# A decoder layer's first norm: x loaded first, its squares summed on PE, c spread by PE, zeros run through PE

## The chip, the core and the metric

The kernel runs on one core of one Trainium2 chip. The metric is the device time of one execution in microseconds. The engines are named as in the profile: PE (matrix products) with PEld (its weight loads), DVE (vector), ACT (activations), POOL (general), SP (which issues the DMAs).

## What is computed

One layer of a hybrid decoder, on 256 rows of width 2048 in float32, conditioned by a vector c:

```python
cond = silu(c)
mod = cond @ ada_w + ada_b                   # nine vectors of 2048: shift, scale, gate for three blocks
h = rmsnorm(x, g1) * (1 + sc1) + sh1
x = x + 0.5 * gt1 * (silu(h @ wg1) * (h @ wu1)) @ wd1          # FFN 1, inner width 5632
h = rmsnorm(x, g2) * (1 + sc2) + sh2
x = x + gt2 * mixer(h)                       # 8 attention heads beside 8 gated-delta heads
h = rmsnorm(x, g3) * (1 + sc3) + sh3
x = x + 0.5 * gt3 * (silu(h @ wg2) * (h @ wu2)) @ wd2          # FFN 2
out = rmsnorm(x, final_norm)
```

rmsnorm divides each row by the root of the mean of its squares plus 1e-6. The change touches only what comes ahead of FFN 1's first matmul: silu(c), the first columns of mod, and the first rmsnorm.

## The kernel before

x is held transposed: 128 partitions, 16 slices (KD) of 128 channels, 256 rows T in the free dimension.

**Weights.** All weight matrices are packed in the order of their use, in blocks of 8 tiles of 128x128 (`Stream.next`, line 84). A block is loaded by SP (`wraw`, line 91), rounded by ACT to float32r (`whi`, line 94), and DVE takes the remainder (`wlo`, line 97). Three buffers of each hold blocks, and a fourth one takes every fourth block of an FFN. The activations are split likewise into a high and a low part (`hs`), so that each product is made of three matmuls: high by high, high by low, low by high.

**Modulation columns.** `mod` is made column by column on DVE (`ada_col`, line 186): SP loads 128x2048 weights, 1 MB (`adaf` for the first four, which have buffers of their own, then `adat`), and one multiply-and-sum against `cs` (silu(c), spread over all partitions) gives one column of 128 values (line 204). The first 32 columns are the scale and the shift of norm 1 in turn, slice by slice. After the first ones they go between the blocks of weights, at a rate per block that the table `RATE` gives.

**The start.** SP issues c, `colt` (small constants, the identity and the ones among them), the first column, x in five parts, three more columns (lines 152 to 162), then the stream. POOL spreads c over the partitions in four pieces (line 175), and ACT takes the silu (line 176). Then come two columns (line 505 on), a load of the Sqrt table (line 240), the squares of x on ACT part by part (line 507), their sum over the slices on DVE down to two slices (lines 506 and 509), and `norm_rstd` (line 255): four fp32 matmuls against two columns of ones (`nsum`, line 261), the root on ACT, reciprocal and one correction on DVE, the result laid out as `rb` (line 275), and two matmuls with the identity which make of it a row on all partitions (`nrow`, line 276), copied by DVE (line 281). `modulate_one` (line 286) makes a slice of h: `ht` on DVE (line 289), shift and rounding on ACT (lines 291, 292, 295), the low part on DVE (lines 293, 296). It needs a scale column (`gains`, line 298) and a shift column.

**FFN 1's first half.** `gate_up_first` (line 400) makes products in chunks of slices k (0 to 1, 2 to 5, 6 to 15) for 28 pairs of gate and up tiles. In the first chunk, eight pairs do k = 0 (two blocks of weights), then k = 1 (two blocks), then the others pair by pair; ACT evacuates each pair's PSUM bank (line 436). The matmuls are those of lines 423 to 425 (`pgu`).

**Order.** A scheduler places the instructions of each engine into one fixed order, by readiness; each engine then works strictly through its list. `tc.issue_after(i)` keeps an instruction behind i in that order. `W.hold` and `W.held` are such marks for the first `wlo`.

## Time and profile before

| | |
|---|---|
| median of 3 runs | 2117.76 us (2116.71 to 2119.72) |
| the profiled execution's own time | 2118.8 us |
| its span in the trace | 2117.0 us |
| mean granted clock of PE | 0.989 |
| first matmul of FFN 1 (`pgu`) | at 27.03 us |
| first matmul with a `wlo` | at 32.36 us |

A row of the trace in order of time reads: start in us, duration in us, engine, line, operation, output<-inputs, shapes, count, and in brackets how long the engine had been idle before and what released it. A row of a stretch reads: from:to and its length, then the busy us and the instructions of PE, PEld, DVE, ACT and POOL, the granted clock of PE, the share of time in which the DMA engines were busy, and GB/s. A row of a group ends with its count, busy us, mean ns of one, and idle us before.

### The profile page before, as it was taken

The numbers are of one execution on the slowest core, as the hardware profiler recorded it, in microseconds if no ns is written. First come the engines' busy times: TensorE is split into PE (matmuls) and PEld (weight loads), VectorE is DVE, ScalarE is ACT, GpSimd is POOL, SyncE is SP. The second block draws the span as 40 slices with busy tenths as digits, with TensorE's granted clock in tenths as the row PEclk, the third lists the DMA queues.
The fourth block names the chain that finished last, engine by engine and source line by source line (L and its number), as shares of the span: only waits on it lengthen the run. The fifth ranks groups of instructions, "written<-read, shape, count | busy, mean of one in ns | idle before, by whom it ended". The sixth has DMA issues, their size and how long they took to land.

```text
span 2117.0 us, 32815 instructions
## 1 busy us (share of the span) xinstructions
PE 2042.3 (96%) x12530; PEld 1808.7 (85%) x12530; DVE 1604.4 (76%) x2580; ACT 1021.3 (48%) x1622; POOL 99.7 (5%) x113
## 2 busy tenths in 40 slices
PE   5999999999999998999999999999999999999997
PEld 4998999888888887788888888788888888888886
DVE  6899877888888878789888888776665555555554
ACT  5544444433444446565556654554444334444442
POOL 0000000000000020110101002100000000000011
PEclk9999999999999999999999999999999999999998
DMA  8989776999999884655555557576666556555553
GB/s 313 331 341 348 265 253 254 334 349 333 331 334 328 339 290 154 202 209 200 196 203 212 197 219 282 192 262 230 234 234 197 188 187 191 191 190 189 189 189 110
DMA packets 123582, 518.16 MB, mean 245 GB/s; under 512 B 13721, under 2 KB 15769, under 8 KB 104993
## 3 DMA queue, kind: packets, MB, share of 16 engines
q1 hardware_dynamic: 123426, 516.07, 69.3%
q8 instruction: 98, 1.61, 0.3%
q14 instruction: 58, 0.48, 0.1%
HBM read 511.81 MB, written 4.21 MB: 244 GB/s over the span
## 4 chain that ended last, share of the span: by engine, by line
PE 82%; DVE 9%; DMA 4%; issue 2%; ACT 2%; POOL 0%; DVEq 0%; SPq 0%; ACTq 0%
PE pd L353 15%; PE pg L353 10%; PE pu L353 10%; PE pd L354 8%; PE pp L353 6%; PE pu L354 5%; PE pg L354 5%; PE pgu L425 4%; PE pgu L423 3%; PE pgu L424 3%; PE pp L354 3%; DVE wlo L97 3%; PE po L353 2%; DVE adat L204 2%; DMA adat<-in_ada_dram 2%
## 5 line engine op out<-in xcount | busy, mean ns | idle before, releaser
L94 ACT CAST whi<-wraw 128x1024 fp32r<-128x1024 f32 x674 | 705.9, 1049 | 802.6 <-PE pd L353 220.7
L97 DVE TENSOR_TENSOR wlo<-wraw,whi 128x1024 fp32r<-128x1024 f32 x674 | 823.3, 1225 | 349.2 <-ACT whi L94 348.0
L353 PE MATMUL pd<-hid,whi 128*128 128x512 f32 x1408 | 492.2, 393 | 0.0
L354 PE MATMUL pd<-hid,wlo 128*128 128x256 f32 x1408 | 393.2, 279 | 0.3 <-DVE wlo L97 0.3
L204 DVE CUSTOM_DVE_ANT_0 adat<-adat,cs,colt 128x2048 f32<-128x2048 f32 x140 | 334.6, 2390 | 42.1 <-DMA adat<-in_ada_dram 41.5
L353 PE MATMUL pg<-hs,whi 128*128 128x512 f32 x960 | 339.9, 394 | 2.6 <-DVE hs L296 1.8
L353 PE MATMUL pu<-hs,whi 128*128 128x512 f32 x960 | 340.3, 395 | 0.0
L353 PEld LDWEIGHTS pd<-hid,whi 128*128 128x128 f32 x1408 | 263.7, 187 | 61.9 <-DVE hid L368 0.3
L353 PE MATMUL pp<-hs,whi 128*128 128x512 f32 x784 | 292.9, 407 | 1.8 <-DVE hs L296 1.8
L354 PE MATMUL pu<-hs,wlo 128*128 128x256 f32 x960 | 269.5, 281 | 0.0
L354 PE MATMUL pg<-hs,wlo 128*128 128x256 f32 x960 | 269.4, 281 | 0.0
L354 PEld LDWEIGHTS pd<-hid,wlo 128*128 128x128 f32 x1408 | 264.4, 188 | 0.7 <-DVE wlo L97 0.6
L423 PE MATMUL pgu<-hs,whi 128*128 128x256 f32 x896 | 255.9, 287 | 8.0 <-ACT whi L94 6.9
L425 PE MATMUL pgu<-hs,wlo 128*128 128x256 f32 x896 | 252.1, 287 | 7.3 <-DVE wlo L97 7.1
L424 PE MATMUL pgu<-hs,whi 128*128 128x256 f32 x896 | 255.1, 286 | 0.0
L354 PE MATMUL pp<-hs,wlo 128*128 128x256 f32 x784 | 230.1, 294 | 0.2 <-DVE wlo L97 0.2
L353 PEld LDWEIGHTS pg<-hs,whi 128*128 128x128 f32 x960 | 180.6, 188 | 44.1 <-issue 2.1
L353 PEld LDWEIGHTS pu<-hs,whi 128*128 128x128 f32 x960 | 180.6, 188 | 41.4
L354 PEld LDWEIGHTS pg<-hs,wlo 128*128 128x128 f32 x960 | 181.9, 189 | 0.5 <-DVE wlo L97 0.4
L423 PEld LDWEIGHTS pgu<-hs,whi 128*128 128x128 f32 x896 | 174.2, 195 | 9.4 <-ACT whi L94 7.8
L354 PEld LDWEIGHTS pu<-hs,wlo 128*128 128x128 f32 x960 | 182.0, 190 | 0.1
L425 PEld LDWEIGHTS pgu<-hs,wlo 128*128 128x128 f32 x896 | 171.8, 194 | 9.3 <-DVE wlo L97 9.2
(269 smaller groups left out, 2197.4 us busy)
## 6 DMA issues: line engine op xcount, KB each, us to landing
wraw<-in_w_dram SPq DMA_DIRECT2D x674, 512.0 KB, 4.4
adat<-in_ada_dram SPq DMA_DIRECT2D x140, 1024.0 KB, 6.9
adaf<-in_ada_dram SPq DMA_DIRECT2D x4, 1024.0 KB, 12.7
xd<-x SPq DMA_DIRECT2D x4, 512.0 KB, 6.4
rw<-rows SPq DMA_DIRECT2D x16, 128.0 KB, 6.2
x<-xd SPq DMA_DIRECT2D x4, 512.0 KB, 7.1
out_dram<-o SPq DMA_DIRECT2D x8, 256.0 KB, 2.2
x<-in_x_dram SPq DMA_DIRECT2D x3, 512.0 KB, 7.8
```

The costliest lines, as they stand in the source:

```text
L94: nc.scalar.copy(self.h, r)
L97: nc.vector.tensor_tensor(self.l, r, self.h.bitcast(F32), ALU.subtract)
L204: V.tensor_tensor_reduce(t, t, cs, 1.0, L("adab", q, 1), ALU.mult, ALU.add, mod[:, q : q + 1])
L353: PE.matmul(ps, wt[0], act.rearrange("p a t -> p (a t)"), start=first, stop=False)
L354: PE.matmul(ps[:, :T], wt[1], act[:, 0], start=False, stop=last)
L423: PE.matmul(o, wh, hs[:, k, 0], start=first and s == 0, stop=False, skip_group_check=skip)
L424: PE.matmul(o, wh, hs[:, k, 1], start=False, stop=False, skip_group_check=skip)
L425: PE.matmul(o, wl, hs[:, k, 0], start=False, stop=last, skip_group_check=skip)
```

## The change

In the new code `pgu` is lines 427 to 429, a column is line 210, and what lies behind FFN 1 has line numbers higher by 20.

- SP issues c, x in four equal parts, `colt`, two columns; columns 3 and 4 are issued where they are used, behind the first blocks of weights.
- PE runs ten bf16 matmuls of 512 columns on a tile of zeros (`warm_up`) at the start, and twelve more behind the matmuls of `nrow`. Nothing reads their results.
- All 16 slices of squares go to PE as they come from ACT: 32 fp32 matmuls against two columns of ones. The sums on DVE are gone.
- c is spread by four fp32 matmuls of a row of ones by 512 elements of c (`pcs`), and ACT takes the silu out of PSUM, behind the squares.
- The first norm's root no longer uses ACT's Sqrt: `rsqrt` (which other stages of the kernel had already) makes it on DVE from a guess by the bits and three Newton steps.
- The copy of `nrow` moves from DVE to ACT. Both first columns now stand behind the norm in the program.
- Columns 3 and 4 aren't placed ahead of the first `wlo` any more.

```diff
-X_AT = 1
+N_WARM = (10, 12)
...
+    zw = ep.tile([P, 512], BF16, name="zw")
+    V.memset(zw, 0.0)
+    one = ep.tile([1, P], F32, name="one")
+    V.memset(one, 1.0)
+
+    def warm_up(n):
+        zp = psb("zp")
+        for _ in range(n):
+            PE.matmul(zp, zw[:, :P], zw, start=True, stop=True)
+
+    warm_up(N_WARM[0])
+    crow = ep.tile([1, D], F32, name="crow")
     nc.sync.dma_start(crow, c)
+    x_parts = [slice(4 * i, 4 * i + 4) for i in range(4)]
+    for sl in x_parts:
+        nc.sync.dma_start(x[:, sl], xt[:, sl])
     nc.sync.dma_start(colt, cols)
-    first_ada = []
-    x_parts = [slice(0, 4), slice(4, 8), slice(8, 12), slice(12, 14), slice(14, 16)]
-    for i in range(N_FIRST):
-        if i == X_AT:
-            for sl in x_parts:
-                nc.sync.dma_start(x[:, sl], xt[:, sl])
-        t = ep.tile([P, D], F32, name=f"adaf{i}")
-        nc.sync.dma_start(t, adaw[i])
-        first_ada.append(t)
+    first_ada = [ep.tile([P, D], F32, name=f"adaf{i}") for i in range(N_FIRST)]
+    for i in range(2):
+        nc.sync.dma_start(first_ada[i], adaw[i])
...
-    for q in range(4):
-        sl = slice(q * 512, (q + 1) * 512)
-        G.partition_broadcast(cs[:, sl], crow[:, sl])
-        A.activation(cs[:, sl], cs[:, sl], AF.Silu)
...
         if first_ada:
             t = first_ada.pop(0)
+            if i >= 2:
+                nc.sync.dma_start(t, adaw[i])
...
-        W.hold, W.held = ada_done[0, 0]().ins, []
-        for _ in range(2, N_FIRST):
-            ada_col()
+        W.hold, W.held = None, [ada_done[0, 0]().ins]
...
     xsq = ep.tile([P, KD, T], F32, name="xsq")
+    ps = psf("nsum")
+    for sl in x_parts:
+        sq = A.activation(xsq[:, sl], x[:, sl], AF.Square)
+        for k in range(sl.start, sl.stop):
+            for t in range(2):
+                PE.matmul(ps[:, t * 2 : t * 2 + 2], xsq[:, k, t * P : (t + 1) * P], L("ones", 0, 2),
+                          start=(k == 0 and t == 0), stop=(k == KD - 1), skip_group_check=True)
+
+    for q in range(4):
+        sl = slice(q * 512, (q + 1) * 512)
+        pcs = psn(q + 3, "pcs")
+        PE.matmul(pcs, one, crow[:, sl], start=True, stop=True)
+        with tc.issue_after(sq.ins):
+            A.activation(cs[:, sl], pcs, AF.Silu)
+    fv = ep.tile([P, 2], F32, name="fv")
+    V.tensor_scalar(fv, ps[:, 0:4:2], 1.0 / D, EPS, ALU.mult, ALU.add)
+    fy = rsqrt(fv, 2, "n")
+    frb = ep.tile([P, 2, P], F32, name="frb")
+    pr = psf("nrow")
+    for t in range(2):
+        V.tensor_scalar(frb[:, t], L("ones"), fy[:, t : t + 1], None, ALU.mult)
+        nr = PE.matmul(pr[:, t * P : (t + 1) * P], frb[:, t], ident, start=True, stop=True)
+    with tc.issue_after(nr.ins):
+        warm_up(N_WARM[1])
+    first_row = tmp.tile([P, T], F32, name="nrow", bufs=1)
+    A.copy(first_row, pr[:, :T])
     for _ in range(2):
         ada_col()
-    tc.keep_in_program_order(sqrt_table(cs[:, :1]))
-    for q, sl in enumerate(x_parts):
-        n = sl.stop - sl.start
-        if q == 3:
-            V.tensor_add(xsq[:, :n], xsq[:, :n], xsq[:, n : 2 * n])
-        A.activation(xsq[:, sl], x[:, sl], AF.Square)
-        if q:
-            W.hold = V.tensor_add(xsq[:, :n], xsq[:, :n], xsq[:, sl]).ins
-    sqa["src"] = [xsq[:, k] for k in range(2)]
-    first_row = norm_rstd(keep_row=True)
     early.close()
```

`rsqrt` as it stood, for DVE:

```python
        eng.tensor_scalar(hv, v, -0.5, None, ALU.mult)
        eng.tensor_scalar(ai, v.bitcast(I32), 1, None, ALU.logical_shift_right)
        eng.tensor_scalar(yi, ai, -1.0, float(MAGIC), ALU.mult, ALU.add)
        for _ in range(3):
            eng.tensor_tensor(a, y, y, ALU.mult)
            eng.tensor_tensor(a, a, hv, ALU.mult)
            if eng is V:
                eng.scalar_tensor_tensor(y, a, 1.5, y, ALU.add, ALU.mult)
```

More of the change, by code (lines that the diff above doesn't have):

```diff
@@ L147, in layer_kernel @@
     ep = early.enter_context(tc.tile_pool(name="early", bufs=1))
-    crow = ep.tile([1, D], F32, name="crow")
     warm = ep.tile([P, 1], F32, name="warm")
```

## Prediction

> **What bounds the kernel now.** I read the page's first block, then the busy times by stretch, then the instructions in order of time at the start, because every line of the diff runs ahead of the first FFN.

> ```profile
> span 2117.0 us, 32815 instructions
> PE 2042.3 (96%) x12530; PEld 1808.7 (85%) x12530; DVE 1604.4 (76%) x2580; ACT 1021.3 (48%) x1622; POOL 99.7 (5%) x113
> ```
> ```profile
> 20.00:30.00 10.00, 5.96 (x26) 5.58 (x26) 8.13 (x15) 3.60 (x5) 0.00 (x0) 1.00 0.70 286
> 30.00:40.00 10.00, 8.02 (x53) 7.73 (x53) 8.79 (x12) 2.92 (x5) 0.00 (x0) 0.83 0.65 265
> 40.00:60.00 20.00, 20.00 (x169) 20.00 (x169) 16.05 (x18) 16.54 (x28) 0.00 (x0) 1.00 0.89 321
> ...
> 100.00:150.00 50.00, 48.08 (x395) 47.20 (x394) 49.62 (x61) 20.41 (x24) 0.00 (x0) 1.00 0.87 323
> 150.00:200.00 50.00, 47.06 (x387) 46.16 (x385) 47.85 (x56) 17.18 (x21) 0.00 (x0) 1.00 0.94 349
> ```

> PE is the bound overall. After 40 us it never stops for 20 us (169 matmuls, 0.118 us each); from 100 to 200 us DVE is 97% busy and PE idles 4.9 us. Up to 40 us PE has mostly waited. So the change can win or lose only by moving the point at which PE runs without a break, and later stages should pass that shift on one for one. As marker I take the end of weight block 3 (blocks hold 8 tiles, each with 3 matmuls: 96 matmuls). By 40.0 us PE has issued 14 + 53 = 67 of them (the first stretch's other rows are nsum and nrow), so block 3 ends at 40.0 + 29 x 0.118 = 43.4 us.

> ```profile
> 8.08 2.80 POOL L175 PARTITION_BROADCAST cs<-crow  x4 [7.64 <-issue]
> ...
> 11.57 2.35 DVE L204 CUSTOM_DVE_ANT_0 adaf<-adaf,cs,colt 128x2048 f32<-128x2048 f32 x1 [10.71 <-ACT cs L176]
> ...
> 19.77 2.35 DVE L204 CUSTOM_DVE_ANT_0 adaf<-adaf,cs,colt 128x2048 f32<-128x2048 f32 x1
> 19.90 1.78 PEld L261 LDWEIGHTS nsum<-colt,xsq 128*128 128x128 f32 x8 [19.90 <-DVE xsq L509]
> ...
> 22.37 0.16 DVE L269 TENSOR_TENSOR nya<-nstd 128x2 f32<-128x2 f32 x1
> 22.56 0.16 DVE L270 TENSOR_TENSOR nya<-nya,nhv 128x2 f32<-128x2 f32 x1
> ...
> 22.96 0.48 DVE L275 TENSOR_SCALAR rb<-colt,nstd 128x128 f32<-128x128 f32 x2
> ...
> 23.30 1.22 PE L276 MATMUL nrow<-colt,rb 128*128 128x128 f32 x4 [1.53 <-DVE rb L275]
> 24.55 0.42 DVE L281 COPY nrow<-nrow 128x256 f32<-128x256 f32 x1 [1.12 <-PE nrow L276]
> ...
> 25.54 0.51 ACT L295 ACTIVATE hs<-ht,mod 128x256 fp32r<-128x256 f32 x1 [3.46 <-DVE ht L289]
> ...
> 26.08 0.48 DVE L296 SCALAR_TENSOR_TENSOR hs<-ht,mod,hs 128x256 fp32r<-128x256 f32 x1 [0.57 <-ACT hs L295]
> 26.48 2.34 DVE L204 CUSTOM_DVE_ANT_0 adaf<-adaf,cs,colt 128x2048 f32<-128x2048 f32 x1
> ...
> 28.75 2.35 DVE L204 CUSTOM_DVE_ANT_0 adaf<-adaf,cs,colt 128x2048 f32<-128x2048 f32 x1
> ...
> 31.02 0.15 DVE L302 SCALAR_TENSOR_TENSOR g<-mod,colt 128x1 f32<-128x1 f32 x1
> 31.09 1.22 DVE L97 TENSOR_TENSOR wlo<-wraw,whi 128x1024 fp32r<-128x1024 f32 x1
> 32.23 0.48 DVE L289 SCALAR_TENSOR_TENSOR ht<-x,g,nrow 128x256 f32<-128x256 f32 x1
> 32.36 0.19 PEld L425 LDWEIGHTS pgu<-hs,wlo 128*128 128x128 f32 x1 [2.27 <-DVE wlo L97]
> ...
> 33.76 0.42 DVE L293 TENSOR_TENSOR hs<-ht,hs 128x256 fp32r<-128x256 f32 x1
> ...
> 37.50 1.22 DVE L97 TENSOR_TENSOR wlo<-wraw,whi 128x1024 fp32r<-128x1024 f32 x1
> ```

> Two modulation columns cost DVE 2.35 us each. The first runs at 11.57, once POOL has spread c; the second hides under the wait for nsum at 19.77. Only eight nsum halves (four fp32 matmuls, two halves each) follow the squares' sum on DVE. Then the row is spread, h0 is split at 26.08, two more columns go ahead of the first wlo, and PE stands until 32.36.

> **The change part by part.** Let N be the moment at which the last nsum matmul ends (21.8 now).

> *Loads.* The queue now carries c, x in four parts, colt, two columns, two weight blocks, two columns, a block, a column, a block. nsum needs colt (its ones), so that x and colt, 2.42 MB, come first.

> ```profile
> GB/s 0 100 376 390 330 358 399 421 434 410 421 404 426 404 404 437 429 328 36 0 0 0 224 464 374 410 429 437 382 333 210 325 205 382 314 109 371 404 391 284
> ```
> ```profile
> adaf<-in_ada_dram SPq DMA_DIRECT2D x1, 1024.0 KB, 5.7
> ```

> The slices are 1.5 us. Their sum passes 2.42 MB at 9.2 us. The first column of before, 1.37 MB deep in the same sum, is passed at 6.2 and landed at 1.55 + 5.7 = 7.25, 1.05 later. So colt lands at about 10.2. The last square (1.05 us for a part) is ready before its turn. The columns land in time: 4.52 MB at 15.3, 7.66 MB at 23.

> *PE ahead of nsum.* Ten zero matmuls and three of the four pcs lie in the wait for colt. No row shows them. From the fp32 rows below, 128 more columns cost 0.098 us a half, so 512 cost about 0.4, a pcs 0.8, at half speed 1.6; a zero matmul is at most twice the 0.235 us that 512 columns need at 0.118 for 256. Ending between 6 and 11 us, they cost nothing, at worst 0.8.

> ```profile
> L860 PE MATMUL plog<-x 128*128 128x256 f32 x16 | 4.8, 380 | 0.0
> ...
> L860 PE MATMUL plog<-x 128*128 128x128 f32 x16 | 3.2, 282 | 0.3 <-DVE x L361 0.3
> ```

> *nsum.* It grows from 8 halves to 64, behind colt, while the sums on DVE (4.7 us) go. This term decides. The row above gives (1.78 - 0.33) / 7 = 0.207 us a half; a later norm, with PE at full clock, gives (0.53 - 0.19) / 3 = 0.113:

> ```profile
> 796.11 0.53 PEld L261 LDWEIGHTS nsum<-colt,sqacc 128*128 128x128 f32 x4
> ```

> So nsum lasts 7.2 to 13.2 us, and N is 17.4 to 23.4. Everything queues behind it: pcs 4 and nrow on PE, and on DVE, whose next instruction is fv, both columns and all wlo.

> ```profile
> 27.62 0.41 PE L423 MATMUL pgu<-hs,whi 128*128 128x256 f32 x1
> 27.84 0.41 PE L424 MATMUL pgu<-hs,whi 128*128 128x256 f32 x1
> ...
> 33.06 0.28 PE L423 MATMUL pgu<-hs,whi 128*128 128x256 f32 x1
> ...
> 33.19 0.28 PE L424 MATMUL pgu<-hs,whi 128*128 128x256 f32 x1
> ```

> The first matmuls of the FFN come 0.21 us apart, and after 3 us of them and a pause 0.12 to 0.13. So 5 us or more of zeros and pcs should have raised the clock by 10 us; whether two-column matmuls hold it no row shows. I take the middle, 0.16 (full clock at first, half later): N = 20.4.
> [...]

> *From N to the end of block 3*, in the order that the scheduler now gives each engine. DVE does fv and twelve rsqrt operations, 13 x 0.195 (the distance of L269 and L270) instead of five: +2.6. frb: +3.1. Both columns now stand behind the norm, since the fourth pcs follows nsum on PE: the first to +5.5, g and ht to +6.1, the second to +8.5 (2.27 from one to the next). nrow (1.23) and its copy, now on ACT, lie beside them. ACT's h0 is ready at +9.1, where PE starts; DVE's at +9.5. wlo0 and wlo1 (1.15 apart) come directly behind: +11.8. PE does blocks 0 and 1 (48 x 0.12) by +14.9 and waits for h1, which takes two more columns, g, ht, wlo2: +18.6. Then column, g, ht, wlo3: +22.6. PE needs 2.5 us for the rest of block 2, 8 matmuls of block 3, then wlo3 and 16 more: +24.6 with a full clock.

> ```profile
> 33.00:34.00 1.00, 1.00 (x9) 1.00 (x9) 1.00 (x2) 0.97 (x3) 0.00 (x0) 0.88 0.40 143
> 34.00:35.00 1.00, 1.00 (x6) 1.00 (x6) 1.00 (x2) 0.64 (x1) 0.00 (x0) 0.50 1.01 401
> ```

> Now a pause of 2.0 us before 32.36 is followed by half clock from 33.9. The new pause between +14.9 and +18.1 is longer; it may cost block 2 up to 1.2 us, of which wlo3 hides half: +25.2. I take +24.9. The twelve zero matmuls behind nrow end by +10 even at half speed; that pause absorbs it.
> [...]

> *ACT's order.* whi of block 5 now stands behind the evacuation of the ninth bank instead of the eighth.

> ```profile
> 38.95 0.59 ACT L436 COPY acc<-pgu 128x512 f32<-128x512 f32 x1 [4.31 <-PE pgu L425]
> 39.43 1.05 ACT L94 CAST whi<-wraw 128x1024 fp32r<-128x1024 f32 x1
> ```

> That bank is done 12 matmuls into block 4. Copy 0.59, cast 1.05, wlo 1.2 follow, about 2.9 us against 16 matmuls (1.9 us) until PE needs wlo5: a stall of 0.9, bounded by 0 and 1.5.

> *Costing nothing*: four POOL broadcasts (POOL idle after them), and ACT's table load of 1.3 us, which no longer comes before the squares; ACT is 29% busy from 30 to 40 us.

> Sum: 20.4 + 24.9 + 0.9 - 43.4 = **+2.8 us**. The profiled execution took 2118.8 (1.8 around its span); the median, 2117.8, is 1.0 below it. On the median I predict **2120.6**, 0.13% slower, inside the 0.2% (4.2 us) that a measurement of this kernel can tell from no change.

> **The rivals.**
> *PE keeps its full clock through nsum.* N = 17.4: 17.4 + 25.8 - 43.4 = -0.2, 2117.6. For it: halves follow each other without a gap, so PE looks busy. Against it: 2 columns in 0.113 us are little work, and the trace's half clock came although PE was at work from 32.36 on.
> [...]

> *PE runs nsum at half speed nearly throughout*, because the zeros don't raise the clock or the wait for colt loses it. Above 0.181 us a half the loss passes 4.2 us; at 0.207 it is 23.4 + 25.8 - 43.4 = +5.8, 2123.6. For it: the only early nsum in the trace ran so, and PE may pause 1 to 3 us before colt. Against it: PE is busy for 5 us or more just before.

> *Faster.* Loads near the best slice (464 GB/s) from the start bring colt by 8.5, the clock holds (N = 15.7), and neither pause nor whi5 costs: 15.7 + 24.6 - 43.4 = -3.1. Past -4.2 it needs back some of the 4.9 us that PE idles between 100 and 200. Against: DVE's work there is the same.

> **How the numbers follow.** Forecast (halves of 0.136 to 0.181, +1.2 to +4.2): 0.40. Clock held: 0.25. Half speed: 0.28. Faster by over 4.2 us: 0.07. So faster 0.07, same 0.65, slower 0.28. The range takes in the -0.2 and the +5.8 with the bounds of the small terms (0 to 0.8 ahead of nsum, 0.3 either way on the pause, 0 to 1.5 on whi5): 2115.5 to 2124.5.

> **What would show it.** Right: first nsum at 10 to 11 us, last at about 20, ht at N + 6, first pgu at N + 9, a pause of 3 us ahead of h1, the 96th pgu matmul near 46. Wrong: halves of 0.113 to the end, a marker before 42, or a shift at the marker that has changed by 200 us.

## The result, and the profile after

The changed kernel takes **2132.06 us** in the median (2131.66 to 2133.61); the kernel before, run beside it, takes 2117.24 (2115.47 to 2119.72). The ratio is 1.0067, with an interval of 1.0054 to 1.0079: 14.2 us slower, where 2.8 were forecast. The profiled execution took 2131.72 us, 2.2 of them around its span.

The page's first block shows 12.5 us more span, and 31 us more of PE being "busy":

```profile
span 2129.5 us, 32976 instructions
...
PE 2073.0 (97%) x12615; PEld 1827.4 (86%) x12616; DVE 1602.3 (75%) x2584; ACT 1019.8 (48%) x1618; POOL 97.7 (5%) x109
```

Busy time by stretch, the answer to the rows of before:

```profile
0.00:10.00 10.00, 6.67 (x16) 2.31 (x16) 0.46 (x3) 5.22 (x6) 0.20 (x4) 0.89 0.79 280
10.00:20.00 10.00, 9.67 (x46) 9.70 (x46) 0.00 (x0) 1.95 (x4) 0.00 (x0) 0.50 1.02 426
20.00:30.00 10.00, 8.87 (x30) 6.23 (x31) 5.29 (x19) 1.91 (x3) 0.00 (x0) 0.50 0.65 271
30.00:40.00 10.00, 8.84 (x56) 6.70 (x54) 9.35 (x11) 2.40 (x3) 0.00 (x0) 0.91 0.44 165
40.00:60.00 20.00, 17.27 (x125) 16.70 (x126) 17.00 (x20) 13.46 (x23) 0.00 (x0) 0.91 0.75 257
```

PE now looks busy from the start, but from 10 to 30 us at a granted clock of 0.50, and DVE does nothing at all from 10 to 20 us. From 40 to 60 us PE does 125 matmuls, where it did 169. The same stretch in order of time:

```profile
1.22 3.91 PE L160 MATMUL zp<-zw 128*128 128x512 bf16 x10 [1.22 <-DVE zw L153]
...
5.05 2.84 PE L515 MATMUL pcs<-crow,one 1*128 1x512 f32 x6
...
10.30 13.73 PEld L509 LDWEIGHTS nsum<-colt,xsq 128*128 128x128 f32 x64 [3.23 <-issue]
10.33 13.79 PE L509 MATMUL nsum<-colt,xsq 128*128 128x2 f32 x64 [2.44 <-DMA colt<-in_cols_dram]
...
24.15 0.16 DVE L519 TENSOR_SCALAR fv<-nsum 128x2 f32<-128x2 f32 x1 [22.86 <-PE nsum L509]
...
29.64 0.48 DVE L295 SCALAR_TENSOR_TENSOR ht<-x,g,nrow 128x256 f32<-128x256 f32 x1
...
33.00 0.39 PE L427 MATMUL pgu<-hs,whi 128*128 128x256 f32 x1 [0.38 <-ACT hs L301]
...
42.02 1.01 PE L427 MATMUL pgu<-hs,whi 128*128 128x256 f32 x3 [2.80 <-ACT hs L298]
...
49.20 0.28 PE L429 MATMUL pgu<-hs,wlo 128*128 128x256 f32 x1
...
52.60 0.38 PE L427 MATMUL pgu<-hs,whi 128*128 128x256 f32 x1 [0.19 <-ACT whi L94]
...
53.86 0.19 PEld L429 LDWEIGHTS pgu<-hs,wlo 128*128 128x128 f32 x1 [0.73 <-DVE wlo L97]
```

The loads do what was forecast: colt lands, and nsum begins, at 10.3. But its 64 halves take 13.73 us, 0.2145 each, and N is 24.1. DVE has waited 22.86 us for that. The row at 49.20 is the 96th pgu matmul.

To follow the shift further, take one row that both kernels have. The `wlo` of the fourteenth block stands in the same surroundings in both (a wait of 0.21 or 0.22 us for `whi`). Before, then after:

```profile
67.09 1.23 DVE L97 TENSOR_TENSOR wlo<-wraw,whi 128x1024 fp32r<-128x1024 f32 x1 [0.21 <-ACT whi L94]
```
```profile
74.50 1.23 DVE L97 TENSOR_TENSOR wlo<-wraw,whi 128x1024 fp32r<-128x1024 f32 x1 [0.22 <-ACT whi L94]
```

**The front costs 7.4 us**, half of the loss. I call this distance the front shift below. The other half shows far behind the diff, where PE never stops. Here are three stretches inside the second half of FFN 1 and both halves of FFN 2, where only gate and up products run; before, then after:

```profile
560.00:690.00 130.00, 130.00 (x751) 114.53 (x750) 112.53 (x131) 63.05 (x94) 0.00 (x0) 1.00 0.92 332
1400.00:1580.00 180.00, 180.00 (x1025) 156.73 (x1024) 119.10 (x144) 85.66 (x129) 0.00 (x0) 1.00 0.69 234
1760.00:1960.00 200.00, 200.00 (x1154) 176.14 (x1153) 114.04 (x145) 96.31 (x144) 0.00 (x0) 1.00 0.59 190
```
```profile
560.00:690.00 130.00, 130.00 (x738) 112.82 (x737) 110.32 (x129) 62.54 (x93) 0.00 (x0) 1.00 0.90 330
1400.00:1580.00 180.00, 180.00 (x1021) 156.09 (x1020) 120.80 (x148) 86.24 (x130) 0.00 (x0) 1.00 0.69 237
1760.00:1960.00 200.00, 200.00 (x1134) 173.49 (x1134) 112.45 (x142) 94.27 (x143) 0.00 (x0) 1.00 0.58 187
```

PE is 100% busy at full clock in all six rows, and yet issues 738 matmuls instead of 751. A weight tile takes two matmuls here (512 and 256 columns), so that it costs 346 ns before (130 us / 751 x 2) and 352 after. Read from one tile to the next, in the trace, the figures are 347 and 353; the expectations below use those. This is **a pace, not a wait**: no idle time shows it, only the count does.

It has a price: 1.76% of some 165 us (the products that the first row is cut from), 0.4% of some 235 and 1.76% of some 235 us make 2.9 + 0.9 + 4.1 = 7.9 us. With the 7.4 of the front that is 15.3, against 14.2 measured (11.4 to 16.7 by the interval).

What did the change do there? `rsqrt` takes three small tiles, `rsy`, `rsa` and `rsh`, with two buffers of 32 bytes each, out of a pool that lives as long as the kernel. Everything that is placed behind this pool then lies 192 bytes higher: the products of FFN 1 and 2 (`hid`, `acc`) and the buffers that take every fourth weight block (`wraw`, `whi`, `wlo`).

### The profile page after: what moved, and what is told of

Same layout as the page of the kernel before. It is cut to its first block, busy times and chain, and to the rows that moved or that the text cites. A ratio compares the mean times of both kernels' runs of the same rounds, so it can differ in the third digit from the quotient of the medians.

```text
span 2129.5 us, 32976 instructions
## 1 busy us (share of the span) xinstructions
PE 2073.0 (97%) x12615; PEld 1827.4 (86%) x12616; DVE 1602.3 (75%) x2584; ACT 1019.8 (48%) x1618; POOL 97.7 (5%) x109
## 4 chain that ended last, share of the span: by engine, by line
PE 82%; DVE 9%; DMA 4%; ACT 2%; issue 2%; POOL 0%; SPq 0%; DVEq 0%; ACTq 0%
PE pd L359 15%; PE pg L359 10%; PE pu L359 10%; PE pd L360 8%; PE pp L359 6%; PE pg L360 5%; PE pu L360 5%; PE pgu L429 3%; PE pgu L427 3%; PE pgu L428 3%; PE pp L360 3%; DVE wlo L97 3%; DMA adat<-in_ada_dram 2%; PE po L359 2%; DVE adat L210 2%
## 5 line engine op out<-in xcount | busy, mean ns | idle before, releaser
L94 ACT CAST whi<-wraw 128x1024 fp32r<-128x1024 f32 x674 | 706.1, 1049 | 804.6 <-issue 221.6
L97 DVE TENSOR_TENSOR wlo<-wraw,whi 128x1024 fp32r<-128x1024 f32 x674 | 824.0, 1227 | 344.0 <-ACT whi L94 341.2
L359 PE MATMUL pg<-hs,whi 128*128 128x512 f32 x960 | 344.6, 399 | 2.4 <-DVE hs L302 1.8
## 6 DMA issues: line engine op xcount, KB each, us to landing
adat<-in_ada_dram SPq DMA_DIRECT2D x140, 1024.0 KB, 7.0
adaf<-in_ada_dram SPq DMA_DIRECT2D x4, 1024.0 KB, 10.8
```

The costliest lines, as they stand in the source:

```text
L94: nc.scalar.copy(self.h, r)
L97: nc.vector.tensor_tensor(self.l, r, self.h.bitcast(F32), ALU.subtract)
L359: PE.matmul(ps, wt[0], act.rearrange("p a t -> p (a t)"), start=first, stop=False)
```

## The experiments

**Theory.** Two causes, which add up. (a) nsum's 64 halves run at half clock throughout, and all else in the front follows nsum, as forecast. (b) The 192 bytes slow the gate and up products. **Rivals.** To (a): what hurts is the new order behind nsum, or the two columns there, not the number of halves. To (b): the longer program, the PSUM banks that the new tiles have shifted, or the later front itself. The shift of each run is that of the fourteenth `wlo`, its pace the count of matmuls from 560 to 690 us.

### Squares summed on DVE again

```diff
-        for k in range(sl.start, sl.stop):
-            for t in range(2):
-                PE.matmul(ps[:, t * 2 : t * 2 + 2], xsq[:, k, t * P : (t + 1) * P], L("ones", 0, 2), ...
+        if q:
+            V.tensor_add(xsq[:, :4], xsq[:, :4], xsq[:, sl])
+    V.tensor_add(xsq[:, :2], xsq[:, :2], xsq[:, 2:4])
+    for k in range(2):
+        for t in range(2):
+            PE.matmul(ps[:, t * 2 : t * 2 + 2], xsq[:, k, t * P : (t + 1) * P], L("ones", 0, 2), ...
```

> The changed kernel, with the squares of x summed on DVE again (three adds of 1024, one of 512) and four nsum matmuls instead of 32; all else as changed. Theory (nsum's 64 halves at half speed are the front's loss): nsum ends at about 14.3 us instead of 24.1, and the weight blocks from the 16th on stand 2.4 us ahead of the kernel before instead of 7.4 behind. Rival (the two columns behind the norm, or the new order of ACT, is the loss): nsum ends earlier, but the blocks still stand 3 us or more behind. Of the time: 2115 if the slower pace of FFN matmuls (353 ns a tile instead of 347) comes with nsum's instructions, 2122 if it stays.

2119.83 us (2117.9 to 2123.3), ratio 1.0018 (1.0008 to 1.0027): 12 us below the changed kernel. Its fourteenth `wlo`:

```profile
64.25 1.23 DVE L97 TENSOR_TENSOR wlo<-wraw,whi 128x1024 fp32r<-128x1024 f32 x1 [0.21 <-ACT whi L94]
```

The front is now 2.8 us *ahead* of before, though loads, pcs, rsqrt, columns and zeros are all those of the change. So the order behind nsum isn't what hurts; the 64 halves are. It is still slower than before, since its products run at the slow pace (739 matmuls from 560 to 690 us). The time lies between the two that were expected: 2.8 us gained and some 8 lost would be 5 above before, and the interval is 1.7 to 5.7.

### More zeros ahead of nsum, pcs behind it

```diff
-N_WARM = (10, 12)
+N_WARM = (34, 12)
...
-        PE.matmul(pcs, one, crow[:, sl], start=True, stop=True)
+        with tc.issue_after(ns.ins):
+            PE.matmul(pcs, one, crow[:, sl], start=True, stop=True)
```

> The changed kernel with 34 zero matmuls at the start, up to the landing of colt, and the four matmuls that spread c behind nsum, so that PE enters nsum at full clock. If two-column matmuls hold the clock, nsum lasts 7.2 us and ends near 17.5. If they don't, the clock falls within 3 to 7 us of nsum's start and nsum ends between 19.5 and 22.5. The rest of the front gets longer, since c is spread later (about 4 us); the time is not read.

One execution: 2132.65 us. nsum, and the clock in it:

```profile
10.29 9.97 PEld L509 LDWEIGHTS nsum<-colt,xsq 128*128 128x128 f32 x64 [0.60 <-issue]
```
```profile
13.00:14.00 1.00, 1.00 (x11) 1.00 (x11) 0.00 (x0) 0.00 (x0) 0.00 (x0) 1.00 0.98 414
14.00:15.00 1.00, 1.00 (x9) 1.00 (x8) 0.00 (x0) 0.00 (x0) 0.00 (x0) 0.73 0.96 393
15.00:16.00 1.00, 1.00 (x7) 1.00 (x6) 0.00 (x0) 0.00 (x0) 0.00 (x0) 0.50 1.03 422
```

Here the clock is up when nsum begins, and falls at about 14.5 (0.73 is 0.46 us at 1.00 and the rest at 0.50), 4.2 us into a row of matmuls without a gap. So these matmuls of two columns didn't hold it. N is 20.3, inside the 19.5 to 22.5 that was expected. The time didn't follow, because all four pcs now run behind nsum, at half clock (0.90 us a half): the columns, and with them the first pgu, come later than in the changed kernel (34.0 against 33.0). This run says nothing on the price of N.

### The kernel before with 192 bytes taken

```diff
+    for nm in ("rsy", "rsa", "rsh"):
+        V.memset(tiny.tile([P, 2], F32, name=nm + "_n", tag=nm + "n"), 0.0)
```

> The kernel before, with three more tiny tiles (two buffers each) that nothing reads: all that is placed behind them lies 192 bytes higher, as in the changed kernel; three tiny memsets on DVE are added. If the slower pace in the FFNs comes from the addresses, gate and up tiles of FFN 1's second half take 353 ns instead of 347, and the time is about 2124. If it comes from PE's instructions ahead, 347 ns stay and the time is 2117.

2126.06 us (2122.66 to 2127.99), ratio 1.0036 (1.0023 to 1.0048): 7.6 us for tiles that nothing reads.

```profile
560.00:690.00 130.00, 130.00 (x738) 112.82 (x738) 111.01 (x130) 62.29 (x92) 0.00 (x0) 1.00 0.91 330
```

738, as in the changed kernel, and 1134 from 1760 to 1960. Theory (b) holds: the place of tiles alone makes the pace, in a kernel whose work and front are those of before (three tiny memsets apart).

### The kernel before with 86 zero matmuls at its start

```diff
+    zw = ep.tile([P, P], BF16, name="zw")
+    V.memset(zw, 0.0)
+    for n in (30, 28, 28):
+        zp = psb("zp")
+        for _ in range(n):
+            PE.matmul(zp[:, :P], zw, zw, start=True, stop=True)
```

> The kernel before, with 86 matmuls on zeros (128 columns) ahead of everything on PE, in the time in which PE waits anyway: as many pairs as the changed kernel has more than the one before. Addresses behind the start stay. If the slower pace in the FFNs follows from how many instructions PE has run before, gate and up tiles of FFN 1's second half take 353 ns instead of 347 and the time is about 2123; if it comes from addresses, 347 ns and 2117, or 1 less since the clock is up for nsum.

2120.38 us (2117.32 to 2122.51), ratio 1.0011 (0.9999 to 1.0023), front shift 0.5.

```profile
560.00:690.00 130.00, 130.00 (x751) 114.52 (x750) 112.54 (x130) 63.33 (x95) 0.00 (x0) 1.00 0.92 336
```

751: a longer program doesn't slow the products. The time was expected at 2117 or 1 less. It is some 2 us above that, by an interval that just takes in no change; the clock that its zeros raised falls at 12.8 (0.64 in the mean from 10 to 20 us), before nsum, whose halves take 0.214 again.

### The change with its tiles at their old places

```diff
-    def rsqrt(v, n, name, eng=V, parts=P):
+    def rsqrt(v, n, name, eng=V, parts=P, pool=tiny):
...
-        y = tiny.tile([P, n], F32, name="rsy_" + name, tag="rsy" + name)
+        y = pool.tile([P, n], F32, name="rsy_" + name, tag="rsy" + name)
...
-    fy = rsqrt(fv, 2, "n")
+    fy = rsqrt(fv, 2, "n", pool=ep)
```

> The changed kernel with only the three small tiles of the first rsqrt taken from the early pool, so that every tile of the FFNs stands at its address of before; work, order and front are those of the changed kernel. Theory (the 192 bytes slow the gate and up products, the front is a loss of its own): front shift stays +7.4 us, a tile of the gate and up products goes back from 353 to 347 ns (351.8 in the first half of FFN 2), the shift no longer grows at 540 to 700 and 1740 to 1975 us, time 2124 to 2126. Rival (something else of the change, PSUM banks or the length of the program, slows them): 353 stays, 2132.

2124.52 us (2120.28 to 2128.31), ratio 1.0026 (1.0014 to 1.0038): 7.5 us below the changed kernel. One tile pool in one call takes back half of the loss.

```profile
560.00:690.00 130.00, 130.00 (x751) 114.49 (x750) 112.57 (x132) 63.98 (x95) 0.00 (x0) 1.00 0.90 335
```
```profile
1.22 4.45 PE L160 MATMUL zp<-zw 128*128 128x512 bf16 x10 [1.22 <-DVE zw L153]
...
5.59 5.49 PE L515 MATMUL pcs<-crow,one 1*128 1x512 f32 x6
...
74.43 1.23 DVE L97 TENSOR_TENSOR wlo<-wraw,whi 128x1024 fp32r<-128x1024 f32 x1 [0.21 <-ACT whi L94]
```

The pace of before is back and the front shift stays at 7.3: the two causes are separate, and the rival (PSUM banks, which are those of the change) falls. One thing was not expected: in this execution the ten zeros did not raise the clock at all. They take 4.45 us instead of 3.91, and pcs 0.92 us a half instead of 0.47. nsum begins later (11.0), and N is 24.8.

### Both mended

The last edit and the first together: sums on DVE, tiles at their old places (the "second run" in this text is the one with the sums on DVE).

> The same, and the squares summed on DVE as in the second run of these experiments (four nsum matmuls). Theory: front shift -2.8 us and nothing added later: 2114 to 2116, 0.1 to 0.2% faster than before. Rival (the early gain is given back later because DVE or the loads bind at 100 to 200 us): 2117 to 2118 though the products keep 347 ns a tile.

2113.45 us (2108.95 to 2115.54), ratio **0.9973** (0.9962 to 0.9985): faster than before, by 5.7 us (3.2 to 8.1), where 0.1 to 0.2% was expected. Its fourteenth `wlo`, and a stretch of FFN 2's first half:

```profile
65.49 1.23 DVE L97 TENSOR_TENSOR wlo<-wraw,whi 128x1024 fp32r<-128x1024 f32 x1 [0.21 <-ACT whi L94]
```
```profile
1400.00:1580.00 180.00, 180.00 (x1039) 158.53 (x1038) 121.21 (x147) 87.11 (x130) 0.00 (x0) 1.00 0.68 237
```

The front is 1.6 us ahead of before. It was 2.8 with the sums on DVE alone; 1.2 are lost because in this execution the clock fell after the pause of 3 us ahead of h1 (pgu matmuls 0.21 us apart for some 3 us behind it, against 0.12 with the sums on DVE alone). From 1400 to 1580 us PE did 1039 matmuls, 14 more than before; this is taken up at the end. The front alone doesn't account for the 5.7 us. The profiled execution is the fastest of seven, and the other pace from 1400 to 1580 us gave it some 3 us; how many of the others had that pace isn't known.

### Which tiles make the pace

Three runs of the kernel before, one execution each, with gaps put between pools. In the first, only the buffers of the fourth weight block lie 192 bytes higher:

```diff
+        with tc.tile_pool(name=f"gapa{which}", bufs=1) as ga, \
+                tc.tile_pool(name=f"hid{which}", bufs=PARTS[which][1] + HIDX) as hp, \
+                tc.tile_pool(name=f"gapb{which}", bufs=1) as gb, \
...
+            for p_, n_ in ((ga, 0), (gb, 192)):
```

> The kernel before with only the buffers of the fourth weight block (wraw, whi, wlo) 192 bytes higher; hid, acc and the rest keep their places. If the place of these weights makes the slower pace: 353 ns a tile of gate and up, about 2121 to 2126. If it is the place of hid or of the evacuated products: 347 ns, 2117 to 2118.

In the second, the gaps are 192 bytes ahead of `hid` and 3904 behind it:

> The kernel before with only hid and acc (where gate and up products go) 192 bytes higher, and the fourth weight block's buffers 4096 bytes higher. If the place of hid makes the slower pace: 353 ns a tile of gate and up; if that of the weights counts, and only in its low digits: 347 ns, 2117 to 2118; if a move of the weights by any distance counts, neither 347 nor 353.

And a third one has a gap of 64 bytes ahead of the weights alone:

> The kernel before with only the fourth weight block's buffers 64 bytes higher instead of 192. If any move off the old place slows the gate and up products: 353 ns a tile. If the step is coarser: 347 ns as before. A value between would mean that the pace depends on the low digits of the address in more than two steps.

2133.45, 2119.74 and 2118.89 us. The weights 192 bytes higher, then `hid` higher with the weights 4096 higher, then the weights 64 higher:

```profile
560.00:690.00 130.00, 130.00 (x739) 112.82 (x738) 110.20 (x129) 62.60 (x93) 0.00 (x0) 1.00 0.90 329
```
```profile
560.00:690.00 130.00, 130.00 (x751) 114.48 (x751) 111.82 (x130) 63.55 (x94) 0.00 (x0) 1.00 0.91 334
```
```profile
560.00:690.00 130.00, 130.00 (x750) 114.37 (x750) 112.54 (x131) 63.36 (x94) 0.00 (x0) 1.00 0.92 335
```

It is the place of the fourth block's weights: 192 bytes slow the products, 64 and 4096 don't, so it seems to be the low digits of the address that count. The first of the three took more time than the 2121 to 2126 expected: against before, it is 4 us behind by 215 us already, where the kernel with 192 bytes taken, whose products are as slow, is 0.4 ahead. Why is open; the verdict rests on the counts. Why a shift of one buffer in four slows them stays open: in the changed kernel's trace, 137 of the 367 distances from tile to tile between 560 and 690 us are 358 to 361 ns and the others 345 to 350, two to four of any eight in a row, so that the long ones run through all blocks, not only that one (before, all are 346 to 352).

### Clock held up to nsum

On the change with its tiles at their old places: pcs ahead of nsum, zeros between.

```diff
-N_WARM = (10, 12)
+N_WARM = (12, 12)
+N_MID = 2
...
+    for q in range(4):
+        with tc.issue_after(zl.ins):
+            zl = PE.matmul(pcs, one, crow[:, sl], start=True, stop=True)
+        with tc.issue_after(zl.ins):
+            zl = warm_up(N_MID, zp0)[1]
```

> The changed kernel, tiles at their old places, all four pcs ahead of nsum with two zero matmuls of 512 columns behind each (and twelve ahead instead of ten); nsum keeps its 64 halves on PE. Theory (the clock fell because pcs, one row deep, and then two idle us did not hold it; two-column matmuls lose it again after some 4 us): nsum starts at 10.3 to 11.0, its halves run at 0.113 for about 4 us and at 0.21 behind that, the last ends near 20.2, the front shift is +3 to +4 us instead of +7.4, time 2120 to 2122. Rival 1 (the squares' sums are slow on PE whatever the clock): last nsum at 24, +7, 2124 to 2125. Rival 2 (the front's loss sits behind nsum, in the columns): last nsum at 20 but the shift stays at +6 or more.

2128.86 us (2127.03 to 2129.44), ratio 1.0056 (1.0041 to 1.0071). Neither the theory nor a rival: the run missed its aim.

```profile
8.00:9.00 1.00, 1.00 (x4) 0.11 (x2) 0.00 (x0) 0.80 (x2) 0.00 (x0) 0.80 1.00 400
```
```profile
14.77 13.99 PEld L521 LDWEIGHTS nsum<-colt,xsq 128*128 128x128 f32 x64 [0.28 <-issue]
...
80.41 1.23 DVE L98 TENSOR_TENSOR wlo<-wraw,whi 128x1024 fp32r<-128x1024 f32 x1 [0.21 <-ACT whi L95]
```

The clock fell at 8.6, in the middle of pcs, zeros or not, and the rest of pcs and zeros held nsum up until 14.8. But N = 28.8 gives a front shift of 13.3, and that is worth having: 4.7 us later than in the changed kernel, the front follows by 5.9. (The total is some 12 us above before, less than the front; the profiled execution, too, had 1039 matmuls from 1400 to 1580 us.)

### The clock's own price, with c spread by POOL

Since pcs spoiled both attempts, it is taken out: c goes over POOL as before, and PE has nothing but zeros ahead of nsum, 34 or none.

```diff
-        pcs = psn(q + 3, "pcs")
-        PE.matmul(pcs, one, crow[:, sl], start=True, stop=True)
+        nc.gpsimd.partition_broadcast(cs[:, sl], crow[:, sl])
...
-N_WARM = (10, 12)
+N_WARM = (34, 12)
```

> The changed kernel, tiles at their old places, c spread by POOL as before, 34 zero matmuls ahead of nsum, which is all that PE has there. Theory (pcs let the clock fall, two-column matmuls keep it for some 4 us; the front follows the last nsum one for one): halves of 0.113 to about 14 us and 0.21 from there, the last near 20.2 instead of 24.1, front shift +3 to +4, time 2120.5 to 2122. Rival (the front's loss sits behind nsum): last nsum near 20 and a shift of +6 or more.

> The same without the 34 zeros, so that PE comes to nsum at half clock. Theory: 64 halves of 0.21, the last at 23.9 to 24.2, front shift +7 to +7.5, 2124 to 2125, 3.5 to 4 us above the run beside it. Rival (nsum raises the clock by itself, so that zeros matter little): halves fall to 0.113 after some 4 us and the last comes at 19 to 20.

2120.88 us (2116.64 to 2124.15), ratio 1.0009 (0.9994 to 1.0023), and 2127.16 (2123.97 to 2131.32), ratio 1.0039 (1.0021 to 1.0057). With zeros, then without:

```profile
11.05 11.71 PEld L509 LDWEIGHTS nsum<-colt,xsq 128*128 128x128 f32 x64
...
73.24 1.23 DVE L97 TENSOR_TENSOR wlo<-wraw,whi 128x1024 fp32r<-128x1024 f32 x1 [0.21 <-ACT whi L94]
```
```profile
10.12 13.72 PEld L509 LDWEIGHTS nsum<-colt,xsq 128*128 128x128 f32 x64 [10.12 <-issue]
...
74.47 1.23 DVE L97 TENSOR_TENSOR wlo<-wraw,whi 128x1024 fp32r<-128x1024 f32 x1 [0.21 <-ACT whi L94]
```
```profile
10.00:12.00 2.00, 1.85 (x9) 1.88 (x10) 0.00 (x0) 1.68 (x4) 2.00 (x4) 1.00 0.98 414
```

Without zeros, nsum stays at 0.214 for all of its 13.7 us: these two-column matmuls didn't raise the clock either. N is 23.9, the shift 7.4, so pcs had cost next to nothing by itself. With zeros the clock held for the first 20 halves only ((13.73 - 11.71) / (0.2145 - 0.113)), some 2.3 us (the trace has the fall of the clock at 13.54, 2.5 us after nsum's first load). N is 22.8 instead of 20.2, and the front 1.2 us earlier for 1.1 us of N. So the front follows N, one for one between these two. Over the runs that leave the order behind nsum as it is in the change, that holds to 1.2 us: 5.9 for 4.7 above, and with the tiles at their old places N is 0.7 later than in the changed kernel and the front 0.1 earlier. In these the clock behind the pause ahead of h1 differs (last section). A nsum at N = 20 with nothing else moved was not reached. The 6.3 us between the two medians is more than the front's 1.2: the profiled executions part by another 3 us between 150 and 340 us. Why is open. And the run without zeros is 2 us above the 2124 to 2125 expected for it.

### What the zeros and an earlier column bring

On the version with both mended: without any zeros (`N_WARM = (0, 0)`), and in another run with all pcs ahead of nsum, the first column ahead of fv, and the second one behind frb.

```diff
+    ada_col()
     fv = ep.tile([P, 2], F32, name="fv")
+    with tc.issue_after(ada_st["ins"].ins):
+        V.tensor_scalar(fv, ps[:, 0:4:2], 1.0 / D, EPS, ALU.mult, ALU.add)
...
-    for _ in range(2):
+    with tc.issue_after(fr.ins):
         ada_col()
```

> The sums on DVE and tiles at their old places, without any zero matmul. Theory (the zeros only set the clock, and on this path only eight halves of nsum, nrow and the first blocks feel it): nsum's halves stay 0.21, the first gate and up matmuls run at 0.21 to 0.24 instead of 0.12 for about 3 us, front shift -0.5 to -2 us, time 2113 to 2116. Rival (the zeros bring the gain): shift 0 or above, 2117 or more.

> The sums on DVE and tiles at their old places, as in the sixth of these runs, and besides all four pcs ahead of nsum and the first column on DVE ahead of fv, in the two microseconds in which DVE waits there. Theory (DVE's chain of columns sets the front): wlo of block 0 about 0.9 us sooner than in the sixth run, front shift -2.5 to -3.5, time 2111 to 2113.5. Rival (PE or the loads bind): no difference to the sixth run, 2113 to 2114.

("The sixth run" is the one with both mended.) Without zeros: 2113.19 us (2110.59 to 2117.92), ratio 0.9980 (0.9970 to 0.9991), no loss to the version with them, and a front shift of -2.8, more than the -0.5 to -2 expected. The first gate and up products do run at half clock, 0.21 us apart until 27.85 us and 0.12 behind it, but the pause ahead of h1 takes that up: it is 1.0 us from start to start, against 3.2 with the sums on DVE alone. With the early column: **2110.32 us** (2108.36 to 2111.35), ratio **0.9967** (0.9954 to 0.9980), the best version here. The early column in it, and the fourteenth `wlo`:

```profile
12.83 2.35 DVE L211 CUSTOM_DVE_ANT_0 adaf<-adaf,cs,colt 128x2048 f32<-128x2048 f32 x1 [0.39 <-DMA adaf<-in_ada_dram]
...
62.23 1.23 DVE L97 TENSOR_TENSOR wlo<-wraw,whi 128x1024 fp32r<-128x1024 f32 x1 [0.21 <-ACT whi L94]
```

The column fills DVE's wait for nsum. wlo of block 0 comes at 21.7, 1.6 us sooner than with both mended alone (23.3), and the front shift is -4.9 instead of -1.6. That is more than expected: besides the 1.6, ACT's order now has `whi` of block 5 in time, and from the 120th to the 192nd pgu matmul PE takes 8.6 us instead of 10.0. The total gain of 7 us (4.2 to 9.7) is more than the 4.9 of the front; in the profiled execution the lead grows to 8.0 by 500 us, and why is open. DVE's chain set the front, as the theory had it, and ACT's order behind it.

## Why the prediction was wrong

Step by step, as the prediction put them:

- **Loads**: "colt lands at about 10.2". nsum began at 10.33 with its arrival. Right.
- **nsum**: "I take the middle, 0.16 (full clock at first, half later): N = 20.4". This step failed. It was 0.2145 throughout, N 24.1: 3.7 us. The reason given for the middle, that "5 us or more of zeros and pcs should have raised the clock by 10 us", was half right. The zeros raised it at 4.4, but it fell at 7.9 (the average from 0 to 10 us is 0.89), within pcs. "Half speed nearly throughout", the rival with 0.28, named this case and its N (23.4), and in the front it is what came.
- **From N to the end of block 3**: forecast +24.9. ht came at N + 5.5 (6.1 forecast), the first pgu at N + 8.9 (9.1), h1 after a pause of 2.8 (3.2), and the 96th pgu ended at about 49.3, N + 25.2. Right to 0.3. The 24.9 was the mean of two cases, 24.6 with a full clock and 25.2 with half clock behind the pause. Both occurred: the changed kernel's clock fell there, and with the tiles at their old places it held, with the 96th pgu at N + 24.5.
- **ACT's order**: +0.9 forecast. PE waits at 52.60 and 53.86, where `whi` and `wlo` of block 5 are late: 1.0 us by the distances there. Another 0.8 us goes in small steps until the fourteenth `wlo`; no run separates them. Right in its place, short in size.
- The front's sum, with the measured terms: 24.1 + 25.2 + 1.8 - 43.7 (before's end of block 3, read off the trace) = 7.4. The working held; the one term that was called decisive was mis-sized by 3.7, and two small ones by 1.2 together.
- **"Later stages should pass that shift on one for one"**: this failed too, in a way that the prediction didn't consider. The front's shift was passed on, to within 3 us (from the fourteenth `wlo` to one at 500 us it goes from 7.4 to 6.3 in the changed kernel, from 7.4 to 10.3 in the run without zeros, and why is open), but the products of three stages got slower themselves, by 7 to 8 us. Under "Costing nothing" the small tiles of `rsqrt` don't even stand. The profile of before couldn't show this: there the gate and up products have one place. The diff could have: a helper that allocates from a pool that lives through the kernel moves all that is placed behind it.

So the range failed by the second cause. With the first alone, at N = 24.8, the change costs 5.5 us (3.0 to 8.0, the run with the tiles at their old places), and its 2124.5 stands at the very end of the range. So the range would just about have taken in the mis-sized nsum; it had no room for a cause that the prediction didn't name.

**What the clock column says.** The prediction took 0.207 from before's early nsum, where before's rows have a granted clock of 1.00. In the run without zeros the column reads 1.00 as well while the halves take 0.214. So in these traces the column shows 1.00 until a first change has been recorded (at 4.44 us in the changed kernel's, at 30.34 in before's), and **at the start the pace of the matmuls is the evidence, not the column**. Read so, before's own trace had said it: its first pgu matmuls are 0.21 us apart, where they are 0.12 later, and the halves of its only early nsum took 0.207, where those of a later one took 0.113. Both ran at half speed.

The same ten zeros, at work for 3.9 and 4.5 us, raised the clock at 4.4 in the changed kernel's profile and not at all in that with the tiles at their old places. In these traces the clock changes in steps of 3.41 us (last section). In the changed kernel the zeros filled 3.2 of the 3.41 us ahead of the change at 4.44. With the tiles at their old places the first change comes at 31.15; steps of 3.41 us back from it lead to 3.84 and 7.25, and of no such stretch did the zeros fill more than 2.6 us. So it may be that where the steps lay decided what ten zeros did; no run tests it.

## What to carry to other kernels

Many tiny matmuls are no cheap sum: 64 halves of two columns cost 13.7 us at half clock, the sums on DVE had cost 4.7, and PE looked 97% busy meanwhile. A row that is counted on to keep the clock up must be shown to do so, by the pace of a row like it. And whoever adds even a few bytes to a long-lived pool should compare the matmul counts of a stretch that is never idle, in stages far from the edit, before looking for the cause in the edit.
